# Two of the passes of a down-projection turned into seven-product block multiplication, in one weight stream with the up-projection

## The chip, the core and the metric

The kernel runs on one core of a Trainium2 chip. Its engines work at the same time, each through its own instructions in order: TensorE (PE in the rows) multiplies matrices, VectorE (DVE) and ScalarE (ACT) do elementwise work, GpSimd (POOL) does some elementwise work and issues some transfers, SyncE (SP) issues the other transfers. They wait for each other through semaphores. TensorE reads both operands from the on-chip buffer SBUF and adds its results up in PSUM, whose eight banks VectorE and ScalarE empty. The metric is the device time of one execution in microseconds (us); less is better.

## The reference, cut to what matters

One layer: a state-space group and a convolution group share an input and an output projection, and then a gated MLP with a short convolution follows. All in float32, 512 prompt tokens and 8 x 4 sample tokens, so 544 columns in all.

```python
D_MODEL = 2048
FFN_DIM = ((8 * D_MODEL // 3 + 127) // 128) * 128      # 5504 = 43 tiles of 128
def conv_ffn(h, buf0, w_up, conv_w, conv_b, w_down):
    u = h @ w_up
    u, buf = causal_dwconv(u, buf0, conv_w, conv_b)
    g, v = jnp.split(u, [FFN_DIM], axis=-1)
    return (jax.nn.silu(g) * v) @ w_down, buf
...
f, p_ffc = conv_ffn(rmsnorm(xp, norm_ffn_w[i]), p_ffc0, *ffn_w)
xp = xp + f
...
y_prompt = rmsnorm(xp, norm_final_w)
```

## The kernel before

Everything is held transposed: a tile is 128 features by 544 tokens, stored as two halves of 272 columns. Each float32 product is made from three matmuls. ScalarE rounds a weight block to a high part (`wh`, `sh`), VectorE or GpSimd subtracts to get the low part (`wl`, `sl`), and the input is split in the same way (`Ah`, `Al` and so on); then high x high, high x low and low x high are added up in PSUM. So one 128 x 128 weight tile against both halves of one input tile takes 6 matmuls of 272 columns.

The program is written out by hand in one order; nothing reorders it. It runs through: input projection, state-space and convolution groups, output projection (in `run_jobs`), then the up-projection, then the down-projection, then the final norm.

**Up-projection.** It has 43 groups; group g makes the gate tile and the value tile of feature block g together. The two weight rows (16 input tiles each) are seen as a 2 x 2 matrix of blocks of 8 tiles, the input as 2 x 2 blocks (8 tiles by 272 columns), and the product of the two is made with seven block products in place of eight (Strassen). I call one block product an *item*; its number in the stream is q, its number in its group m. The seven input combinations stand ready in `T_t` (`Ta`, `Th`, `Tl`). The weight combinations are made on the way: of five loads per group two come as a plain load on SP followed by an accumulating load on GpSimd's queue, which adds a second block to the first in SBUF (line 1207); two more sums are made by VectorE (`sum_a` line 1213, `sum_b` line 1217, tile `ws`). The loads sit in five buffers (`wr`). In item q the order is: ScalarE rounds the weights of item q + 2 (`prep_h`), VectorE empties the PSUM bank of item q - 1 (`evac`), a part of the convolution of the group before (`conv_task`), VectorE makes the low part of item q + 2 (`prep_l`), a sum or a load where one is due, and then the 24 matmuls of item q (lines 1250 to 1252). Three buffers for high and three for low parts (`whl`) hold items q, q + 1 and q + 2. Each group ends in a tile of the MLP's hidden layer, which goes to HBM (`ad`).

**Down-projection.** The pools of the up-projection are closed and others opened in their memory (`swap`). The 43 hidden tiles are taken in chunks of 14, 13, 12 and 4 (`CHUNKS`). For each of the first three, the tiles are loaded (`ar`) and split (`Ah`, `Al`, lines 1119 and 1120), and for each of the 16 output tiles the weights come in blocks of up to four tiles (`raw`, `wh`, `wl`, lines 117 and 118), run through `run_jobs` (matmuls on line 228, six for each weight tile), and the sum is added to the residual `xres` (line 1397). The last chunk of four goes through `last_half` with weights kept ready (`kh`, `kl`), one half of the columns after the other, so that the final norm of the first half can run beside the second.

Of the kernel before, what the change touches and what calls it, by code (L numbers as in the profile page):

```python
# [21 lines left out]
CHUNKS = [14, 13, 12, 4]  # L22
# [7 lines left out]
def hymba_step_kernel(ctx: ExitStack, tc: tile.TileContext, a: dict):  # L30
# [236 lines left out]
    with tc.manual_schedule():  # L267
# [833 lines left out]
        def ou_pre(i):  # L1101
            def f():
                if i == 0:
                    while not idle():
                        tick()
                    load_xr(0)
                if i + 1 < 16:
                    load_xr(i + 1)
                else:
                    delay(0, up_open)  # L1110
                    delay(0, lambda: (t_first(5), t_fourth(5)))
                    delay(1, lambda: (t_second(5), t_third(5)))
                    delay(1, lambda: (t_first(6), t_fourth(6)))
                    delay(2, lambda: (t_second(6), t_third(6)))
# [7 lines left out]
        def t_first(k):  # L1122
            t = slot("Ta", dt=F32R)
            split_into(t[:, 0, :], t[:, 1, :], xs[k][:, 0, :])
            T_t[0, k] = (t[:, 0, :], t[:, 1, :])

        def t_pair(k, src, ms):
            h, l = slot("Th", dt=F32R), slot("Tl", dt=F32R)
            split_into(h, l, src)
            for i, m in enumerate(ms):  # L1130
                T_t[m, k] = (h[:, i, :], l[:, i, :])

        tr = {}

        def t_second(k):
            p, q = xs[k], xs[k + 8]
            r = tr[k] = slot("tr")
            V.tensor_tensor(r[:, 1, :], p[:, 0, :], p[:, 1, :], ALU.subtract)
            V.scalar_tensor_tensor(r[:, 0, :], r[:, 1, :], -1.0, q[:, 1, :], ALU.mult, ALU.subtract)
            t_pair(k, r, (2, 3))  # L1140

        def t_third(k):
            p, q = xs[k], xs[k + 8]
            r, s = tr.pop(k), slot("tr")
            V.tensor_tensor(s[:, 0, :], q[:, 1, :], p[:, 1, :], ALU.subtract)
            V.scalar_tensor_tensor(s[:, 1, :], r[:, 0, :], -1.0, q[:, 0, :], ALU.mult, ALU.subtract)
            t_pair(k, s, (4, 6))

        def t_fourth(k):
            t_pair(k, xs[k + 8], (1, 5))  # L1150

        T_STEPS = [t_first, t_fourth, t_second, t_third]
        NPRE = 5

        def ou_evac(i):
            t = OT[i]

            def go(ps):
# [18 lines left out]
                if i % 2 and i // 2 < NPRE:  # L1177
                    steps += [lambda f=f: f(i // 2) for f in T_STEPS]
# [9 lines left out]

        KW = 8 * 128
        raw, wq, wr = {}, {}, None  # L1190

        def up_open():
            nonlocal wr
            wr = swap("wr", "side0", bufs=1, side="right")
            for j in (0, 1, 3, 2, 4):
                load_w(0, j)

        def load_w(g, j):
            if g >= HID:
                return  # L1200
            lo, hi = wup[g], wup[HID + g]
            src = (lo[:, 0:KW], hi[:, 0:KW], lo[:, 0:KW], lo[:, KW:2 * KW], hi[:, KW:2 * KW])[j]
            more = (None, hi[:, KW:2 * KW], hi[:, 0:KW], None, None)[j]
            t = wr.tile([128, KW], F32, tag="r", bufs=5, name=nm("wr"))
            Y.dma_start(out=t, in_=src)
            if more is not None:
                G.dma_start(out=t, in_=more, accum_op=ALU.add)  # L1207
            raw[g, j] = t

        def sum_a(g):  # L1210
            if g < HID:
                raw[g, 5] = wr.tile([128, KW], F32, tag="s", bufs=1, name=nm("ws"))
                V.tensor_tensor(raw[g, 5], raw[g, 1], raw[g, 0], ALU.add)
                load_w(g + 1, 0)

        def sum_b(g):
            V.tensor_tensor(raw[g, 5], raw[g, 5], raw[g, 3], ALU.add)
            load_w(g + 1, 3)

        def prep_h(q):  # L1220
            g, m = divmod(q, 7)
# [412 lines left out]
```

## Time and profile before

| what | value |
|---|---|
| time, median of 3 runs | 2891.84 us (2891.19 to 2894.03) |
| time of the profiled execution | 2892.68 us |
| span of the profiled execution, first to last instruction | 2890.9 us |
| TensorE busy | 2837.0 us, 98% of the span, 22502 matmuls |
| VectorE busy | 1933.7 us, 67% |
| ScalarE busy | 1170.8 us, 40% |
| GpSimd busy | 882.5 us, 31% |
| mean granted TensorE clock | 0.992 of full speed |

Matmuls are pipelined: a matmul's recorded 289 ns covers its way through the array, and the next one starts long before it ends. What a matmul costs is therefore read from the distance of starts, or from the number of matmuls in a stretch without idle time. The profiled execution took 0.84 us more than the median.

### The profile page before, as it was taken

The page shows a single profiled execution, that of the slowest core. Times are in us where ns is not written, and L with a number is a line of the kernel's source. Part 1 is how long each engine was busy: PE and PEld are TensorE (multiplying, and loading weights), DVE is VectorE, ACT ScalarE, POOL GpSimd, SP SyncE. Part 2 cuts the span into 40 slices and gives each one's busy share as a digit, 9 for nine tenths or more (in the row PEclk, how much of TensorE's full clock was granted, in tenths as well). Part 3 has the DMA queues.
Part 4 walks back from the last instruction along what each step waited for, and adds up shares of the span by engine and source line. Part 5 has one row for each costly group of instructions (what it writes and reads, how often), then busy time and mean ns, then how long its engine had stood idle before and what let it go on. Part 6 is the DMA issues. An engine that isn't in the chain of part 4 may idle for free. (4 is left out here: it accounts for less than half of the span.)

```text
span 2890.9 us, 55668 instructions
## 1 busy us (share of the span) xinstructions
PE 2837.0 (98%) x22502; PEld 2796.8 (97%) x22502; DVE 1933.7 (67%) x2912; ACT 1170.8 (40%) x1768; POOL 882.5 (31%) x896
## 2 busy tenths in 40 slices
PE   8999999999999999999999999999999989999997
PEld 7999998999999999999899999999999989999997
DVE  7576665777777778244598888888888863242335
ACT  4545444333333424233344444444444442232224
POOL 4466657667676655401100000000000000000003
PEclk9999999999999999999999999999999999999999
DMA  4243342433333343444476767777677764343521
GB/s 162 83 122 103 90 141 91 128 107 105 103 97 94 102 153 117 142 134 133 142 186 184 198 184 192 191 189 193 185 195 186 193 202 133 105 134 90 152 80 63
DMA packets 196674, 403.43 MB, mean 140 GB/s; under 512 B 38336, under 2 KB 47168, under 8 KB 196416
## 3 DMA queue, kind: packets, MB, share of 16 engines
q1 hardware_dynamic: 184032, 354.78, 40.0%
q0 software_dynamic: 12384, 45.09, 8.0%
q8 instruction: 176, 2.88, 0.4%
q14 instruction: 82, 0.67, 0.1%
HBM read 357.37 MB, written 42.41 MB: 138 GB/s over the span
## 5 line engine op out<-in xcount | busy, mean ns | idle before, releaser
L117 ACT CAST wh<-raw 128x512 fp32r<-128x512 f32 x592 | 355.6, 603 | 867.7 <-PE mm L228 743.7
L1250 PE MATMUL st<-Th,sh 128*128 128x272 f32 x2064 | 596.1, 289 | 1.5 <-ACT sh L1226 1.5
L1252 PE MATMUL st<-Th,sl 128*128 128x272 f32 x2064 | 595.8, 289 | 1.1 <-DVE sl L1235 1.1
L1251 PE MATMUL st<-Tl,sh 128*128 128x272 f32 x2064 | 595.7, 289 | 0.0
L118 POOL TENSOR_TENSOR wl<-raw,wh 128x512 fp32r<-128x512 f32 x336 | 449.9, 1341 | 422.8 <-ACT wh L117 362.6
L228 PE MATMUL mm<-xh,wh 128*128 128x272 f32 x2304 | 487.5, 293 | 7.5 <-ACT xh L312 7.5
L228 PE MATMUL mm<-xl,wh 128*128 128x272 f32 x2304 | 479.5, 289 | 4.5 <-DVE xl L314 4.5
L228 PE MATMUL mm<-xh,wl 128*128 128x272 f32 x2304 | 478.5, 289 | 0.0
L118 DVE TENSOR_TENSOR wl<-raw,wh 128x512 fp32r<-128x512 f32 (+2 forms) x256 | 180.4, 707 | 354.0 <-ACT wh L117 349.3
L1250 PEld LDWEIGHTS st<-Th,sh 128*128 128x128 f32 x2064 | 388.5, 188 | 1.7 <-ACT sh L1226 1.7
L1252 PEld LDWEIGHTS st<-Th,sl 128*128 128x128 f32 x2064 | 388.5, 188 | 1.5 <-DVE sl L1235 1.5
L1251 PEld LDWEIGHTS st<-Tl,sh 128*128 128x128 f32 x2064 | 388.5, 188 | 0.0
L228 PEld LDWEIGHTS mm<-xh,wh 128*128 128x128 f32 x2304 | 365.6, 189 | 20.5 <-issue 10.4
L228 PEld LDWEIGHTS mm<-xl,wh 128*128 128x128 f32 x2304 | 365.4, 188 | 6.0 <-DVE xl L314 6.0
L228 PEld LDWEIGHTS mm<-xh,wl 128*128 128x128 f32 x2304 | 365.4, 188 | 0.0
L1226 ACT CAST sh<-wr 128x1024 fp32r<-128x1024 f32 x215 | 225.4, 1049 | 272.6 <-PE st L1251 262.2
L1207 POOL DMA_DIRECT2D wr<-in_w_up x86 | 74.9, 871 | 828.9 <-DVE pu L1267 534.3
L937 DVE SCALAR_TENSOR_TENSOR ax<-w,cfw,ax 128x512 f32<-128x512 f32 x448 | 302.2, 747 | 5.8 <-ACT ax L913 5.8
L1235 DVE TENSOR_TENSOR sl<-wr,sh 128x1024 fp32r<-128x1024 f32 x215 | 262.5, 1221 | 40.4 <-ACT sh L1226 40.3
L228 PE MATMUL mm<-Ah,wh 128*128 128x272 f32 x1248 | 260.3, 290 | 7.5 <-ACT Ah L1119 7.5
L228 PE MATMUL mm<-Al,wh 128*128 128x272 f32 x1248 | 260.2, 290 | 0.0
L228 PE MATMUL mm<-Ah,wl 128*128 128x272 f32 x1248 | 260.1, 289 | 0.0
(299 smaller groups left out, 4965.8 us busy)
## 6 DMA issues: line engine op xcount, KB each, us to landing
wr<-in_w_up SPq DMA_DIRECT2D x215, 512.0 KB, 4.6
raw<-in_w_in SPq DMA_DIRECT2D x292, 256.0 KB, 3.2
wr<-in_w_up POOLq DMA_DIRECT2D x86, 512.0 KB, 9.2
raw<-in_w_down SPq DMA_DIRECT2D x144, 256.0 KB, 2.7
raw<-in_w_out SPq DMA_DIRECT2D x128, 256.0 KB, 2.9
ad<-ra SPq DMA_DIRECT2D x43, 272.0 KB, 6.9
ar<-ad SPq DMA_DIRECT2D x43, 272.0 KB, 4.1
h<-in_h SPq DMA_DIRECT2D x32, 256.0 KB, 3.5
```

The lines of the kernel that those rows point to most:

```text
L117: S.copy(h[:, :n], r[:, :n])
L118: (cur["wl"] or eng).tensor_tensor(l[:, :n], r[:, :n], h[:, :n].bitcast(F32), ALU.subtract)
L228: T.matmul(o, lhsT=w[:, c], rhs=x[:, hf, :], start=first, stop=last)
L937: V.scalar_tensor_tensor(p, w[:, i:i + 512], wt(i), p, ALU.mult, ALU.add)
L1207: G.dma_start(out=t, in_=more, accum_op=ALU.add)
L1226: S.copy(h, src)
L1235: V.tensor_tensor(l, src, h.bitcast(F32), ALU.subtract)
L1250: T.matmul(out, lhsT=h[:, c], rhs=xh_, start=k == 0, stop=False)
L1251: T.matmul(out, lhsT=h[:, c], rhs=xl_, start=False, stop=False)
L1252: T.matmul(out, lhsT=l[:, c], rhs=xh_, start=False, stop=k == 7)
```

## The change

The weights of the up- and the down-projection become one stream of items through the same buffers (`wr`, `whl`) and PSUM banks (`pst`); the pools are no longer swapped between them. A `Group` is seven items with five loads, as the up-projection had them; a `Plain` is one item of the ordinary kind: one output tile, K weight tiles, both halves, two PSUM banks. `DOWN = [(6, 6), (5, 6), (4, 0)]` replaces `CHUNKS`: a plain pass over 6 hidden tiles (16 items, one for each output tile), then a pass of eight groups over 12 hidden tiles (6 pairs; a group makes output tiles t and t + 8), a plain pass over 5, eight groups over the next 12, a plain pass over 4, and `last_half` over the last 4 as before. So 24 tiles go through block products and 15 through plain passes.

A group's products are added straight to the residual (`down_evac`, scratch tile `pd`). The seven input combinations of a pair of hidden tiles (`prep_pair`, formerly `t_first` to `t_fourth`) are made during the plain pass ahead (`pairs_prep`). Loads of hidden tiles, residual tiles and kept weights hang on item numbers (`at_item`). The program keeps a count of free load buffers (`free`), and each buffer that falls free takes the next load of the whole stream (`issue`). Of a group's five loads the order is now 0, 1, 3, 2, 4 throughout; before, load 2 went ahead of load 3 from the second group on.

```diff
-CHUNKS = [14, 13, 12, 4]
+DOWN = [(6, 6), (5, 6), (4, 0)]
...
+        class Group:
+            def __init__(self, lo, hi, K, T, evac):
+                n = K * 128
+                self.a = (lo[:, 0:n], lo[:, n:2 * n], hi[:, 0:n], hi[:, n:2 * n])
+                self.K, self.T, self.evac, self.q = K, T, evac, len(items)
+                items.extend((self, m) for m in range(7))
+                loads.extend((self, j) for j in (0, 1, 3, 2, 4))
+                sums[self.q - 1] = lambda: sum_a(self)
+                sums[self.q + 2] = lambda: sum_b(self)
+
+        class Plain:
+            def __init__(self, src, K, rhs, evac):
...
+        def issue(n=0):
+            free[0] += n
+            while free[0] and loads:
+                free[0] -= 1
+                o, j = loads.popleft()
+                src, more = o.a, None
+                if type(o) is Group:
+                    a11, a12, a21, a22 = o.a
+                    src, more = ((a11, None), (a21, a22), (a11, a21), (a12, None), (a22, None))[j]
+                t = wr.tile([128, KW], F32, tag="r", bufs=5, name=nm("wr"))[:, 0:o.K * 128]
+                Y.dma_start(out=t, in_=src)
+                if more is not None:
+                    G.dma_start(out=t, in_=more, accum_op=ALU.add)
+                raw[o, j] = t
...
-            if m in (3, 4, 6):
-                load_w(g + 1, {3: 1, 4: 2, 6: 4}[m])
+            if m in (None, 3, 4, 6):
+                issue(1)
...
+            outs = [pst.tile([128, 512], F32, tag="st", name=nm("st"))[:, 0:NH] for _ in range(2 if m is None else 1)]
+            bank[q] = outs
+            if m is None:
+                mms(outs, (0, 1), h, l, o.K, 0, o.K, o.rhs)
+                return
...
-        swap(None, "wr")
-        Cur.side = swap("side2", bufs=NSIDE, side="right")
-        Cur.wp = swap("wp2", "whl", bufs=1)
-        Cur.pmm = swap("pmm2", "pst", bufs=2, space=bass.MemoryType.PSUM)
...
+        def a_prep(ks, q):
+
+            for i, k in enumerate(ks):
+                at_item(q + i - 2, lambda k=k: a_load(k))
+                at_item(q + i, lambda k=k: a_split(k))
...
+        def plain_evac(t):
+            def f(m, *os):
+                for hf, o in enumerate(os):
+                    V.tensor_tensor(xres[t][:, hf, :], o, xres[t][:, hf, :], ALU.add)
+            return f
+
+        def down_evac(t):
...
+                elif m == 1:
+                    V.tensor_tensor(x[:, 0, :], o, x[:, 0, :], ALU.add)
+                    V.tensor_tensor(x[:, 0, :], x[:, 0, :], p[:, 0, :], ALU.add)
+                elif m == 2:
+                    V.tensor_tensor(p[:, 0, :], o, p[:, 0, :], ALU.add)
+                elif m == 3:
+                    V.tensor_tensor(p[:, 1, :], o, p[:, 0, :], ALU.add)
+                    V.tensor_tensor(x[:, 1, :], x[:, 1, :], p[:, 1, :], ALU.add)
+                elif m == 4:
+                    V.tensor_tensor(p, o.unsqueeze(1).to_broadcast([128, 2, NH]), p, ALU.add)
+                    V.tensor_tensor(y, y, p, ALU.subtract)
...
+        def down_group(k0, n, T):
+            for t in range(8):
+                w = [wdn[i, :, k0 * 128:(k0 + 2 * n) * 128] for i in (t, t + 8)]
+                Group(w[0], w[1], n, T, down_evac(t))
+
+        def pairs_prep(k0, n, T, q, step):
+
+            for i in range(n):
+                b = q + int(step * i)
+                for k in (k0 + i, k0 + n + i):
+                    at_item(b, lambda k=k: a_load(k))
+                st = prep_pair(T, i, lambda i=i: ar[k0 + i], lambda i=i: ar[k0 + n + i])
+                for f, d in zip(st, (2, 2, 3, 4)):
+                    at_item(b + d, f)
+                at_item(b + 4, lambda i=i: (ar.pop(k0 + i), ar.pop(k0 + n + i)))
...
+        for c, (n, pn) in enumerate(DOWN):
+            q = len(items)
+            a_prep(range(k0, k0 + n), q - n + 1)
+            down_plain(k0, n)
...
+            if pn:
+                pairs_prep(k0, pn, T_d[c], q, 11 / (pn - 1))
+                down_group(k0, pn, T_d[c])
+                k0 += 2 * pn
...
+        keep_prep(ktail, ntail, len(items) - 16)
```

Three places where the order of the instructions moves. The first is SP's queue, which issues the transfers, at the end of the up-projection. Names: `wr` and `raw` are weight buffers, `ar` a hidden tile read back from its HBM copy `ad`, `out_o_ffc` and `ad<-ra` are stores of the last groups. Before:

```order
L1205 DMA wr_27467<-in_w_up 128x1024
L179 DMA out_o_ffc<-w_27311 128x50
L179 DMA out_o_ffc<-w_27426 128x50
L179 DMA ad_221<-ra_27498 128x544
L179 DMA out_o_ffc<-w_27563 128x50
L101 DMA raw_27805<-in_w_down 128x512
L101 DMA raw_27811<-in_w_down 128x512
L101 DMA raw_27817<-in_w_down 128x512
L101 DMA raw_27823<-in_w_down 128x256
L101 DMA raw_27829<-in_w_down 128x512
L1377 DMA ar_27831<-ad_181 128x544
```

And in the changed kernel at the same place:

```order
L1224 DMA wr_27467<-in_w_up 128x1024
L179 DMA out_o_ffc<-w_27311 128x50
L1224 DMA wr_27535<-in_w_down 128x768
L1363 DMA ar_27572<-ad_181 128x544
L179 DMA out_o_ffc<-w_27426 128x50
L1363 DMA ar_27610<-ad_182 128x544
L1224 DMA wr_27614<-in_w_down 128x768
L1363 DMA ar_27650<-ad_183 128x544
L1224 DMA wr_27654<-in_w_down 128x768
L1224 DMA wr_27657<-in_w_down 128x768
L179 DMA ad_221<-ra_27498 128x544
```

The first weights of the down-projection and the first hidden tiles now stand among the stores of the last two up groups, and no longer behind all of them.

The second is VectorE in the down-projection where the input of the second block pass is prepared. Before, in the same stretch of the down-projection (the second chunk), low parts of weights and of the next hidden tiles alternate, with one addition to the residual for each output tile:

```order
L1397 TENSOR_TENSOR xres_28160<-mm_28162,xres_28160 128x544
L1120 TENSOR_TENSOR Al_28286<-ar_28226,Ah_28285 128x544
L118 TENSOR_TENSOR wl_28295<-raw_28264,wh_28294 128x256
L1120 TENSOR_TENSOR Al_28325<-ar_28258,Ah_28324 128x544
L118 TENSOR_TENSOR wl_28331<-raw_28292,wh_28330 128x512
```

In the changed kernel, two items of the plain pass over 5 tiles (`tr` holds differences of hidden tiles, `Ta`, `Th` and `Tl` the input of the block products):

```order
L1383 TENSOR_TENSOR xres_27967<-st_30471,xres_27967 128x272
L1383 TENSOR_TENSOR xres_27967<-st_30472,xres_27967 128x272
L1144 TENSOR_TENSOR tr_30507<-ar_30327,ar_30325 128x272
L1145 SCALAR_TENSOR_TENSOR tr_30507<-tr_30460,ar_30327 128x272
L1119 TENSOR_TENSOR Tl_30511<-tr_30507,Th_30510 128x544
L1119 TENSOR_TENSOR Ta_30514<-ar_30416,Ta_30514 128x272
L1119 TENSOR_TENSOR Tl_30518<-ar_30418,Th_30517 128x544
L1258 TENSOR_TENSOR sl_30525<-wr_30297,sh_30503 128x640
L1383 TENSOR_TENSOR xres_28034<-st_30529,xres_28034 128x272
L1383 TENSOR_TENSOR xres_28034<-st_30530,xres_28034 128x272
```

Five more instructions stand between one item's emptying of its two banks and the low part `sl` of the item after next.

The third is VectorE in a down-projection group. Before, every output tile of a chunk had this pattern:

```order
L1397 TENSOR_TENSOR xres_29247<-mm_31023,xres_29247 128x544
L118 TENSOR_TENSOR wl_31131<-raw_31114,wh_31130 128x128
L118 TENSOR_TENSOR wl_31161<-raw_31128,wh_31160 128x512
L118 TENSOR_TENSOR wl_31191<-raw_31158,wh_31190 128x512
L118 TENSOR_TENSOR wl_31221<-raw_31188,wh_31220 128x512
```

Now, from the fifth product of one group to the second of the next (line 1236 is `sum_a`):

```order
L1405 TENSOR_TENSOR pd_28824<-st_28913,pd_28824 128x544
L1406 TENSOR_TENSOR xres_28282<-xres_28282,pd_28824 128x544
L1258 TENSOR_TENSOR sl_28936<-wr_28757,sh_28932 128x768
L1408 TENSOR_TENSOR xres_27817<-st_28938,xres_27817 128x272
L1258 TENSOR_TENSOR sl_28960<-wr_28856,sh_28957 128x768
L1236 TENSOR_TENSOR ws_28962<-wr_28828,wr_28757 128x768
L1410 SCALAR_TENSOR_TENSOR xres_28282<-st_28966,xres_28282 128x272
L1258 TENSOR_TENSOR sl_28988<-ws_28962,sh_28985 128x768
L1258 TENSOR_TENSOR sl_29013<-wr_28828,sh_29009 128x768
```

`sum_a` reads `wr_28828`, the load with an accumulating part, and the low part of the same buffer, two instructions on, is what frees it for the next group's accumulating load.

## Rows read from the trace of the kernel before

**Rows 1.** The page, its head and part 1: span, busy us and share of each engine.

```profile
span 2890.9 us, 55668 instructions
...
PE 2837.0 (98%) x22502; PEld 2796.8 (97%) x22502; DVE 1933.7 (67%) x2912; ACT 1170.8 (40%) x1768; POOL 882.5 (31%) x896
```

**Rows 2.** The page, part 5: groups of matmuls; count, busy, mean ns, idle before.

```profile
L1250 PE MATMUL st<-Th,sh 128*128 128x272 f32 x2064 | 596.1, 289 | 1.5 <-ACT sh L1226 1.5
...
L228 PE MATMUL mm<-Ah,wh 128*128 128x272 f32 x1248 | 260.3, 290 | 7.5 <-ACT Ah L1119 7.5
```

**Rows 3.** Busy time in two stretches: up-projection, down-projection; instructions touched (x), clock, DMA share.

```profile
core 0: us, PE busy (x) PEld busy (x) DVE busy (x) ACT busy (x) POOL busy (x), PEclk, DMA share, GB/s
1800.00:2300.00 500.00, 500.00 (x3972) 500.00 (x3971) 435.06 (x639) 239.13 (x308) 41.14 (x48) 1.00 0.72 191
2400.00:2600.00 200.00, 200.00 (x1581) 200.00 (x1580) 69.50 (x114) 51.73 (x95) 0.00 (x0) 1.00 0.41 117
```

**Rows 4.** TensorE's waits from 2200 us to the end: in total, times, longest.

```profile
PE mm L228 <- ACT Ah L1119: 7.5, 1, 7.5
```

**Rows 5.** TensorE in order of time at the switch: start, length, count, idle before.

```profile
2339.48 0.29 PE L1252 MATMUL st<-Th,sl 128*128 128x272 f32 x1
2347.28 0.82 PE L228 MATMUL mm<-Ah,wh 128*128 128x272 f32 x2 [7.51 <-ACT Ah L1119]
...
2352.74 0.65 PE L228 MATMUL mm<-Ah,wl 128*128 128x272 f32 x2
...
2354.43 0.41 PE L228 MATMUL mm<-Al,wh 128*128 128x272 f32 x2
```

**Rows 6.** SP's queue and ScalarE at the switch, in order of time.

```profile
2339.68 2.24 SPq L101 DMA_DIRECT2D raw<-in_w_down  x5
...
2346.59 0.64 ACT L1119 CAST Ah<-ar 128x544 fp32r<-128x544 f32 x1 [0.71 <-DMA ar<-ad]
```

**Rows 7.** VectorE and ScalarE in one up group, in order of time.

```profile
2275.38 1.22 DVE L1213 TENSOR_TENSOR ws<-wr,wr 128x1024 f32<-128x1024 f32 x1
2276.52 0.43 DVE L1275 TENSOR_TENSOR c<-st,c 128x272 f32<-128x272 f32 x1
2276.88 0.69 DVE L1285 TENSOR_TENSOR w<-c,rr 128x512 f32<-128x512 f32 x1
...
2276.71 1.05 ACT L1226 CAST sh<-ws 128x1024 fp32r<-128x1024 f32 x1 [2.50 <-DVE ws L1213]
```

**Rows 8.** VectorE preparing a pair of input tiles ahead of the up-projection, in order of time.

```profile
1408.20 0.71 DVE L1120 TENSOR_TENSOR Tl<-xs,Th 128x544 fp32r<-128x544 f32 x1
1408.84 0.43 DVE L1138 TENSOR_TENSOR tr<-xs 128x272 f32<-128x272 f32 x1
...
1410.51 0.73 DVE L1120 TENSOR_TENSOR Tl<-tr,Th 128x544 fp32r<-128x544 f32 x1 [0.77 <-ACT Th L1119]
1411.15 0.43 DVE L1145 TENSOR_TENSOR tr<-xs,xs 128x272 f32<-128x272 f32 x1
```

**Rows 9.** Transfers of the up-projection: line 1205 on SP, line 1207 on GpSimd, issue to landing.

```profile
2260.57 4.30 SPq L1205 DMA_DIRECT2D wr<-in_w_up  x3
...
2264.96 0.86 POOL L1207 DMA_DIRECT2D wr<-in_w_up  x1 [16.65 <-DVE pu L1267]
...
L1207 POOL DMA_DIRECT2D wr<-in_w_up x48: 862/865/888, 1799.4 to 2289.5; - x48
...
DMA to landing us min/median/max: 7.9/9.2/10.7
...
L1205 SPq DMA_DIRECT2D wr<-in_w_up x117: 327/328/696, 1804.9 to 2297.8; - x117
...
DMA to landing us min/median/max: 3.5/4.6/8.9
```

**Rows 10.** The page, part 6: transfers by line, KB each, median us to landing.

```profile
raw<-in_w_down SPq DMA_DIRECT2D x144, 256.0 KB, 2.7
...
ar<-ad SPq DMA_DIRECT2D x43, 272.0 KB, 4.1
```

More of the change, by code (lines that the diff above doesn't have):

```diff
@@ L1194, in up_open, with sum_a, sum_b, prep_h @@
             wr = swap("wr", "side0", bufs=1, side="right")
[L1195 to L1199, printed above, removed]
[L1200 to L1225 removed]
+            issue()
+        def sum_a(o):
+            raw[o, 5] = wr.tile([128, KW], F32, tag="s", bufs=1, name=nm("ws"))[:, 0:o.K * 128]
+            V.tensor_tensor(raw[o, 5], raw[o, 1], raw[o, 0], ALU.add)
+            issue(1)
+        def sum_b(o):
+            V.tensor_tensor(raw[o, 5], raw[o, 5], raw[o, 3], ALU.add)
+            issue(1)
+        def prep_h(q):
+            if q >= len(items):
+                return
+            o, m = items[q]
+            src = raw[o, 0 if m is None else (0, 3, 5, 1, 2, 5, 4)[m]]
+            h = whl.tile([128, KW], F32R, tag="h", bufs=3, name=nm("sh"))[:, 0:o.K * 128]
             S.copy(h, src)
@@ L1240, in hymba_step_kernel @@
-        bank = {}
+            if m in (None, 3, 4, 6):
+                issue(1)
         def product(q):
-            g, m = divmod(q, 7)
+            o, m = items[q]
             h, l = wq.pop(q)
-            bank[q] = pst.tile([128, 512], F32, tag="st", name=nm("st"))
-            out = bank[q][:, 0:NH]
-            for k in range(8):
-                xh_, xl_ = T_t[m, k]
-                c = slice(k * 128, k * 128 + 128)
-                T.matmul(out, lhsT=h[:, c], rhs=xh_, start=k == 0, stop=False)
-                T.matmul(out, lhsT=h[:, c], rhs=xl_, start=False, stop=False)
-                T.matmul(out, lhsT=l[:, c], rhs=xh_, start=False, stop=k == 7)
@@ L1401, in hymba_step_kernel @@
+        a_prep(range(ktail, HID), len(items) - 16)
         fin = {}
@@ L1523, in hymba_step_kernel @@
-        run_jobs()
+        run_jobs()
+        whl = swap("whl", "wp", bufs=1)
+        pst = swap("pst", "pmm", bufs=4, space=bass.MemoryType.PSUM)
+        x7 = x_pair(7)
+        prep_h(0)
+        prep_l(0)
+        drain_later()
+        x7[0]()
+        prep_h(1)
+        fcw = cload("fcw", [128, 86, 4])
+        fstate = []
+        for i in range(3):
+            n = min(29, 86 - 29 * i)
+            fstate.append(slot("fs", [128, 29, 16]))
+            Y.dma_start(out=fstate[i][:, 0:n, :], in_=a["ffn_state"][:, 29 * i:29 * i + n, :])
@@ new lines, in hymba_step_kernel @@
+        for q in range(len(items)):
+            tick()
+            if q == 0:
+                x7[1]()
+                prep_l(1)
+                x7[2]()
+                sums[-1]()
+            prep_h(q + 2)
+            if q:
+                evac(q - 1)
+            for fn in tasks.pop(q, []):
+                fn()
+            prep_l(q + 2)
+            if q == 1:
+                x7[3]()
+                xs.clear()
+            if q in sums:
+                sums[q]()
+            product(q)
```

268 lines of the change are left out of this document (110 added, 158 removed).

## The prediction, made before the changed kernel was run

> **What bounds the kernel now.** I read the busy times first: TensorE is busy for 98% of the span, no other engine for more than 67% [rows 1]. A busy TensorE need not be at its best, so I counted matmuls in two stretches without idle time. In the up-projection 3972 are touched in 500 us; two of them lie across the edges, so one costs 500 / 3970 = 0.1259 us. In the down-projection it is 200 / 1579 = 0.1267 us. Both are at full clock [rows 3]. The waits say the same from the other side: in the last 690 us TensorE waits for an operand long enough to notice only once, 7.5 us for the first hidden tile of the down-projection [rows 2, 4]; the up-projection's largest group of matmuls shows 1.5 us of idle time over all its 2064 [rows 2]. So here time is the number of matmuls, plus that one place. A saved matmul is saved time as long as VectorE, ScalarE and the transfers keep two items ahead; that is what has to be checked.
>
> **Part 1, the matmuls.** 24 hidden tiles leave the plain form: 24 tiles x 6 matmuls x 16 output tiles = 2304, at 0.1267 us [rows 3] 291.9 us. They come back as 2 passes x 8 groups x 7 products x 6 tiles x 3 = 2016. These are the same lines and the same one-bank form as in the up-projection, so I take its 0.1259 us: 253.9 us. The difference is -38 us. At the plain rate the new ones cost 255.4 us, and the difference would be -36.5 us; these are the two ends. The other 1440 plain matmuls and the 384 of the last four tiles stay.
>
> **Part 2, the switch.** From the last up matmul at 2339.48 us to 2354.43 us there are 33 starts (one, then 16 rows of two), which at full rate take 33 x 0.126 = 4.2 us; they took 14.95 us [rows 5]. So the switch costs 10.8 us: 7.5 us of idle time, and the rest because the first matmuls after it start 5.46 / 24 = 0.23 us apart [rows 5], which is the 1.2 GHz level of the clock after an engine that stood still, against 0.126 us at 2.4 GHz. The cause is order: SP issues the first down weights at 2339.68 us, just after the last up matmul, the hidden tiles come behind them, and the first `Ah` is rounded at 2346.59 us [rows 6]. In the changed kernel nothing is swapped: the first weights stand among the stores of the last up groups, and the first six hidden tiles are loaded in items 294 to 299 and split two items later. Two up items are 2 x 24 x 0.126 = 6.0 us; such a load lands in 4.1 us [rows 10]. Splitting adds one 544-column instruction on VectorE per item, 0.64 us by the distance of starts [rows 8]. VectorE was busy 87% there [rows 3], 2.63 of 3.02 us, so it falls behind by 0.25 us in each of six items, 1.5 us in all, against a lead of one item and more. I take -10.8 us. If the cover fails, this term goes to nothing.
>
> **Part 3, VectorE in the plain passes.** An item of the 6-tile pass lasts 36 x 0.1267 = 4.56 us, of the 5-tile pass 3.80 us. By distances of starts a 272-column instruction takes 0.36 us and a 1024-column one 1.14 us [rows 7], a 544-column one 0.64 us [rows 8]; on the line between the last two, 640 columns take 0.74 and 768 take 0.87 us. Two steps of the preparation of a pair (`second`, `third`) are each two 272-column differences, a wait for ScalarE of 0.77 us and a 544-column subtraction; the trace has one of them, 2.31 us from 1408.84 to 1411.15 us [rows 8]. The other two steps are 0.36 + 0.64. A pair is 5.6 us, one comes every 2.2 items, and each item brings two evacuations (0.72 us) and a low part. First pass: 5.6 + 2.2 x 1.59 = 9.1 us in 10.0 us of matmuls; the last convolution takes some 4.6 us more in the first six items, once. It keeps up. Second pass: 5.6 + 2.2 x 1.46 = 8.8 us in 8.4 us: behind by 0.4 us a pair, some 2 us after five. What waits for it first are the PSUM banks: item q + 1 needs those of q - 1, so VectorE may be behind by 3.80 - 0.72 = 3.1 us. In items in which two steps meet it is about a microsecond further behind. So the stall is from nothing to 3.6 us: the upper end takes recorded lengths (0.44, 0.73, 0.84 us) with no overlap, which makes 9.7 us a pair, 5 x 1.3 - 3.1 after five. I take +1 us, as distances of starts are what this engine did when it was behind. It can't be a gain, since the matmuls are not fewer for it.
>
> **Part 4, the groups.** A group item is 18 matmuls, 2.27 us, a group 15.9 us. VectorE: seven low parts and two sums at 0.87, seven 272-column and two 544-column instructions, 7.8 + 2.5 + 1.3 = 11.6 us. ScalarE has seven roundings of about 0.8 us. Both fit, no cost.
>
> The narrow place is a loop through the accumulating load: the plain load lands, GpSimd adds the second block, `sum_a` uses the buffer, ScalarE rounds the sum, VectorE makes two low parts, and the second of these frees a buffer for the next group's accumulating load. In the up-projection the plain load was issued at 2260.57 us and the accumulation began at 2264.96 us, 4.4 us later; such a one takes 9.2 us (7.9 to 10.7) to land [rows 9], so at 2274.2 us; `sum_a` began at 2275.38 us [rows 7]. That is 1.2 us in hand, in a group of 21.2 us. The blocks are now 384 KB, not 512, but the group is 15.9 us, and a part of a transfer's time does not shrink. Bounds for the plain load are 2.7 us at 256 KB [rows 10] and 4.6 us at 512 KB [rows 9], I take 3.6. For the accumulation they are 9.2 us unscaled and 6.9 us scaled by size; I take 8.0. The rest is 0.87 + 0.8 + 2 x 0.87 and some 0.1 of hand-over, 3.5 us, with ScalarE's 1.05 us scaled [rows 7]. The loop is 15.1 us, between 13.1 and 17.3, against 15.9. So it costs nothing at the value that I take. Where it is longer, the excess comes seven times in each pass, less a stock of about 2.3 us (a low part is due 4.5 us after its item's turn begins and takes 2.2). At 17.3 us: 2 x (7 x 1.4 - 2.3) = 15 us.
>
> The Trainium skill has a rule for such a transfer ("DMA: Bandwidth & Descriptors", section "Anatomy of one DMA — SWDGE (gpsimd) path"): about 2.0 us fixed plus the bytes at 436 GB/s. By it the accumulation takes 2.9 us as an estimate from that page, the loop 10 us, and the time would be the same as my sum. This trace does not bear the rule out, with 7.9 us at the least for 512 KB [rows 9].
>
> Transfers are no bound: a group moves 7 x 0.393 MB in 15.9 us, 173 GB/s; the up-projection ran at 191 GB/s without a wait [rows 3]. The tail after the last matmul, the up-projection and all ahead of it keep their work. The swapped order of loads 2 and 3 comes after the load that the loop needs.
>
> **Sum.** 2892.68 - 37.9 - 10.8 + 1.0 = 2845.0 us for the profiled execution, which was 0.84 us over the median: 2844 us.
>
> **Rivals.** (a) The accumulating loads set the pace of the groups. For it: 1.2 us in hand before, and a period shorter by a quarter. Against it: smaller blocks and fewer other transfers. At a loop of 16.8 us it costs 2 x (7 x 0.9 - 2.3) = 8 us: 2852 us; at the end 2859 us. (b) VectorE comes late in the plain passes by the upper bound: 3.6 in place of 1.0, 2847 us. (c) The change doesn't do all that it says: the stream still stops at the switch, because `Ah` or the first weights come late behind the stores in SP's queue. Then the 10.8 us stay: 2855 us. (d) Slower than before: loads in the groups collide. At the longest landings of the trace, 8.9 and 10.7 us [rows 9], the loop is 23.1 us, the excess 7.2 us, and 2 x (50 - 2.3) = 96 us are added: 2940 us. It ends above the old time from an excess of 3.8 us, a loop of 19.7 us on average in place of 15.1. Such landings were the worst of 117 and of 48, not their mean.
>
> **How the numbers follow.** Forecast (2841 to 2848 us) 0.66, (b) 0.08, (a) 0.16, (c) 0.06, (d) 0.03, and 0.01 for none of these. The range 2841 to 2856 us takes in the forecast with both ends of part 1, all of (b), (c), and about half of (a), some 0.88; that is no more than the ends of the unknown costs need. A measurement of this kernel can tell about 0.2%, 6 us, from no change. All cases but (d) and the far end of what I can't name are faster by more: faster 0.96, within 0.2% 0.01, slower 0.03.
>
> **What would show it.** Part 1: 2016 matmuls on the group lines of the down-projection, 126 ns apart, and 288 matmuls fewer in all. Part 2: no wait for `Ah`, and no fall of the clock at the end of the up-projection. Part 3: short waits of TensorE late in the second plain pass, for VectorE. Rival (a): waits that grow through a block pass and end with it, VectorE idle ahead of `sum_a` until an accumulating load. Rival (c): one wait of several microseconds at the first plain item. I am wrong if TensorE's idle time in the down-projection adds up to more than some 10 us, or if matmuls in the groups are further apart than 0.127 us with no wait ahead of them.

## The result and the profile after

The changed kernel takes 2846.41 us (median of 4 runs, 2844.91 to 2849.48), the kernel before 2891.73 us beside it: a ratio of 0.9843 with a 95% interval of 0.9826 to 0.9860, so 45.3 us less. The forecast was 2844 us with a range of 2841 to 2856 us.

The page of the changed kernel, head and part 1, answers to [rows 1]. TensorE has 288 matmuls fewer, and VectorE 164 us more work:

```profile
span 2847.7 us, 55491 instructions
...
PE 2798.8 (98%) x22214; PEld 2758.7 (97%) x22214; DVE 2097.4 (74%) x3192; ACT 1214.4 (43%) x1792; POOL 910.8 (32%) x928
```

TensorE's waits from 2200 us to the end (total, times, longest) answer to [rows 4]. The one wait of 7.5 us is gone, and four kinds of short waits stand in its place:

```profile
PE st L1276 <- DVE sl L1258: 0.8, 2, 0.4
PE ax L1487 <- POOL sq L1520: 0.4, 1, 0.4
PE st L228 <- ACT Ah L1118: 0.4, 1, 0.4
PE st L228 <- DVE Al L1119: 0.2, 1, 0.2
```

Busy time in the first block pass and in the second plain pass answers to [rows 3]: TensorE is busy throughout, VectorE in 78% and 79% of it, at full clock.

```profile
core 0: us, PE busy (x) PEld busy (x) DVE busy (x) ACT busy (x) POOL busy (x), PEclk, DMA share, GB/s
2417.00:2544.00 127.00, 127.00 (x1009) 127.00 (x1009) 99.16 (x147) 51.11 (x68) 12.21 (x14) 1.00 0.71 176
2544.20:2605.00 60.80, 60.80 (x482) 60.80 (x482) 47.98 (x98) 24.88 (x41) 1.74 (x2) 1.00 0.56 161
```

The page's part 6 (KB each, median us from issue to landing) has the new accumulating loads, which stand on GpSimd's queue: 5.7 us at 384 KB. No such size was in the trace of before.

```profile
wr<-in_w_up POOLq DMA_DIRECT2D x86, 512.0 KB, 8.2
wr<-in_w_down SPq DMA_DIRECT2D x96, 384.0 KB, 3.4
...
wr<-in_w_down POOLq DMA_DIRECT2D x32, 384.0 KB, 5.7
```

Where the time went is easiest to see by stage. The table is worked out from starts of matmuls in the profiled executions: the first of the up-projection, its last, the first on a hidden tile (`Ah`), the first of the last four tiles, and the end of the span. Ahead of the up-projection nothing was changed, yet the profiled executions of this study reach it between 1417.67 and 1421.29 us, the changed kernel last; the comparison therefore starts there. A second profiled execution of the changed kernel (e8, below) takes 1426.58 us from there on.

| us | before | after | e1 (stream only) | e2 (late tiles) | e5a (order) |
|---|---|---|---|---|---|
| up-projection | 920.23 | 921.55 | 922.08 | 920.00 | 920.23 |
| switch, to the first `Ah` | 7.80 | 0.13 | 0.13 | 5.45 | 0.13 |
| first 39 hidden tiles | 477.33 | 437.67 | 474.40 | 438.99 | 436.53 |
| last 4 tiles and end | 66.31 | 67.08 | 66.75 | 67.46 | 67.08 |
| together | 1471.67 | 1426.43 | 1463.36 | 1431.90 | 1423.97 |

Before to after it is -45.2 us: 7.7 at the switch, 39.7 in the 39 tiles, and two losses, 1.3 in the up-projection and 0.8 at the end.

### The profile page after: what moved, and what is told of

Same layout as the page of the kernel before. It is cut to its first block, busy times and chain, and to the rows that moved or that the text cites. A ratio compares the mean times of both kernels' runs of the same rounds, so it can differ in the third digit from the quotient of the medians.

```text
span 2847.7 us, 55491 instructions
## 1 busy us (share of the span) xinstructions
PE 2798.8 (98%) x22214; PEld 2758.7 (97%) x22214; DVE 2097.4 (74%) x3192; ACT 1214.4 (43%) x1792; POOL 910.8 (32%) x928
## 5 line engine op out<-in xcount | busy, mean ns | idle before, releaser
L1276 PE MATMUL st<-Th,sl 128*128 128x272 f32 x2640 | 762.4, 289 | 1.5 <-DVE sl L1258 1.5
L1274 PE MATMUL st<-Th,sh 128*128 128x272 f32 x2640 | 762.5, 289 | 1.5 <-ACT sh L1249 1.5
L1275 PE MATMUL st<-Tl,sh 128*128 128x272 f32 x2640 | 762.0, 289 | 0.0
L1249 ACT CAST sh<-wr 128x1024 fp32r<-128x1024 f32 (+3 forms) x343 | 327.1, 954 | 415.9 <-PE st L1275 338.9
L1276 PEld LDWEIGHTS st<-Th,sl 128*128 128x128 f32 x2640 | 496.9, 188 | 2.4 <-DVE sl L1258 2.4
L1274 PEld LDWEIGHTS st<-Th,sh 128*128 128x128 f32 x2640 | 496.9, 188 | 1.7 <-ACT sh L1249 1.7
L1275 PEld LDWEIGHTS st<-Tl,sh 128*128 128x128 f32 x2640 | 497.0, 188 | 0.0
L1258 DVE TENSOR_TENSOR sl<-wr,sh 128x1024 fp32r<-128x1024 f32 (+3 forms) x343 | 378.0, 1102 | 55.1 <-ACT sh L1249 55.0
L228 PEld LDWEIGHTS mm<-xh,wh 128*128 128x128 f32 x2304 | 366.0, 189 | 20.4 <-issue 10.6
L1249 ACT CAST sh<-ws 128x1024 fp32r<-128x1024 f32 (+1 forms) x118 | 117.1, 992 | 259.3 <-DVE ws L1236 144.7
L1258 DVE TENSOR_TENSOR sl<-ws,sh 128x1024 fp32r<-128x1024 f32 (+1 forms) x118 | 136.0, 1153 | 31.3 <-ACT sh L1249 22.0
```

The lines of the kernel that those rows point to most:

```text
L228: T.matmul(o, lhsT=w[:, c], rhs=x[:, hf, :], start=first, stop=last)
L1249: S.copy(h, src)
L1258: V.tensor_tensor(l, src, h.bitcast(F32), ALU.subtract)
L1274: T.matmul(outs[0], lhsT=h[:, c], rhs=xh_, start=k == 0, stop=False)
L1275: T.matmul(outs[0], lhsT=h[:, c], rhs=xl_, start=False, stop=False)
L1276: T.matmul(outs[0], lhsT=l[:, c], rhs=xh_, start=False, stop=k == o.K - 1)
```

## Experiments on the two gains

**e1, the shared stream without block products.**

```diff
-DOWN = [(6, 6), (5, 6), (4, 0)]
+DOWN = [(8, 0), (8, 0), (8, 0), (8, 0), (7, 0)]
...
-        T_d = [{}, {}]
+        T_d = [{} for _ in DOWN]
```

> The shared stream alone: all 39 hidden tiles ahead of the last four go in plain passes (8, 8, 8, 8, 7 tiles), no block products. The theory says that the change is two gains that add: 288 matmuls fewer in the groups (38 us, of which none is given back) and a switch without its stop (8.3 of 10.8 us in the profile of the changed kernel). So this kernel keeps only the second: 2891.7 - 8.3 = 2883 us (2880 to 2887, as 80 items in five passes have other evacuations than three passes), with the same 22502 matmuls as before. Rival 1, the stream is worth nothing by itself, or costs what it saves: 2892. Rival 2, the switch is worth more than the gap that is seen in it, and the block products less: 2870 or below.

Measured: 2885.40 us (9 runs, 2882.57 to 2888.91), ratio 0.9976 (0.9966 to 0.9986), 7.4 us under before beside it. By stage it is 8.3 us under before. The 22502 matmuls are all there:

```profile
PE 2834.6 (98%) x22502; PEld 2795.7 (97%) x22502; DVE 1952.3 (68%) x2928; ACT 1151.7 (40%) x1672; POOL 883.4 (31%) x896
```

So the two gains add, as the theory had it. The same 39 tiles take 474.40 us here and 437.67 us in the changed kernel: the block products are worth 36.7 us, and 37.9 us against e5a, which has the block products without the small waits at the switch. 477.33 - 474.40 = 2.9 us is what the low clock behind the stop cost before (granted clock 0.50 from 2347.3 to 2352.7 us).

**e2, the first hidden tiles late.** The first six are loaded and split in the item that uses them.

```diff
-            a_prep(range(k0, k0 + n), q - n + 1)
+            if c == 0:
+                for k in range(n):
+                    at_item(q, lambda k=k: a_load(k))
+                for k in range(n):
+                    at_item(q, lambda k=k: a_split(k))
+            else:
+                a_prep(range(k0, k0 + n), q - n + 1)
```

> The changed kernel, but the first six hidden tiles are loaded and split in the item of their first use, instead of six items ahead. The theory says that the stop at the switch came from this order alone and not from the pools that were swapped: it returns with a wait of 6 to 8 us for the first hidden tile and a stretch at the lower clock behind it, 8 to 10 us in all, less the 2.5 us of small waits that the early splits cost: 2846.4 + 6 to 8 = 2853 to 2855 us. Rival, the swap of pools (or the first weights behind the stores) was the cause: no change, 2846 us.

Measured: 2853.73 us (4 runs, 2853.26 to 2854.14), ratio 0.9863 (0.9847 to 0.9880). TensorE and ScalarE of this kernel at the switch, in order of time (start, length, instruction, count, idle before):

```profile
2340.05 0.29 PE L1276 MATMUL st<-Th,sl 128*128 128x272 f32 x1
2345.50 0.82 PE L228 MATMUL st<-Ah,sh 128*128 128x272 f32 x2 [5.16 <-ACT Ah L1118]
...
2347.34 0.65 PE L228 MATMUL st<-Ah,sh 128*128 128x272 f32 x2
2347.79 0.66 PE L228 MATMUL st<-Al,sh 128*128 128x272 f32 x2
...
2344.81 4.18 ACT L1118 CAST Ah<-ar 128x544 fp32r<-128x544 f32 x6 [2.33 <-DMA ar<-ad]
```

The stop is back, with the pools not swapped: ScalarE waits for the hidden tile's transfer, TensorE for ScalarE. Behind it two matmuls take 0.45 us, 0.23 us each, the same low level of the clock as in [rows 5]; the granted clock from 2345.5 to 2350 us is 0.50. The up-projection in front of it takes 920.00 us, so without early splits its small waits are gone too. The late hidden tiles alone are enough for a stop of 5.2 us. The old one was 7.5 us, with five weight loads (2.24 us of SP's queue, [rows 6]) ahead of the first hidden tile; no run separates these 2.3 us. By stage e2 lies 5.5 us over the changed kernel, less than the 7.3 us of the medians; some of the rest lies ahead of the up-projection, where the two kernels are the same.

**e5a and e5, what stayed at the switch.** First the changed kernel in item 297, VectorE and ScalarE, and then TensorE behind them:

```profile
2332.68 0.19 DVE L1317 TENSOR_TENSOR w<-c,nr 128x32 f32<-128x32 f32 x1
2334.50 0.72 DVE L1119 TENSOR_TENSOR Al<-ar,Ah 128x544 fp32r<-128x544 f32 x1 [1.63 <-ACT Ah L1118]
2335.15 1.22 DVE L1258 TENSOR_TENSOR sl<-ws,sh 128x1024 fp32r<-128x1024 f32 x1
...
2333.08 0.85 ACT L1319 ACTIVATE o<-w,fcw 128x560 f32<-128x560 f32 x1
2333.84 0.63 ACT L1118 CAST Ah<-ar 128x544 fp32r<-128x544 f32 x1
...
2335.71 0.29 PE L1275 MATMUL st<-Tl,sh 128*128 128x272 f32 x1
2336.42 0.39 PE L1276 MATMUL st<-Th,sl 128*128 128x272 f32 x1 [0.42 <-DVE sl L1258]
2336.64 0.29 PE L1274 MATMUL st<-Th,sh 128*128 128x272 f32 x1
```

VectorE makes the convolution's input until 2332.87 us. ScalarE works on it (L1319) and only then rounds the hidden tile. VectorE, whose next instruction is that tile's low part, stands still for 1.63 us. Behind it in VectorE's queue is the low part of the up weights, which TensorE needs. The edit changes the order alone: ScalarE rounds the hidden tile ahead of the convolution, and VectorE makes its low part behind that of the weights.

```diff
+        post = {}
+        def a_early(ks, q):
+            for i, k in enumerate(ks):
+                at_item(q + i - 2, lambda k=k: a_load(k))
+                def hi(k=k):
+                    Ah[k], Al[k] = slot("Ah", dt=F32R), slot("Al", dt=F32R)
+                    S.copy(Ah[k], ar[k])
+                def lo(k=k):
+                    V.tensor_tensor(Al[k], ar.pop(k), Ah[k].bitcast(F32), ALU.subtract)
+                tasks.setdefault(q + i, []).insert(0, hi)
+                post.setdefault(q + i, []).append(lo)
...
-            a_prep(range(k0, k0 + n), q - n + 1)
+            (a_prep if c else a_early)(range(k0, k0 + n), q - n + 1)
...
+            for fn in post.pop(q, []):
+                fn()
             product(q)
```

e5 has `q - n + bool(c)` in place of `q - n + 1`: the first pass one item earlier. e8 is the changed kernel again, on the same chip.

> The changed kernel unaltered, as the measure for the two kernels on the switch that run on the same chip. Both theories expect 2846 us (2844 to 2849), with two waits for low parts of up weights at the end of the up-projection, one for the sixth first-pass tile's Ah and one for its Al.

> The changed kernel with another order within the six items that split the first hidden tiles: ScalarE rounds the hidden tile ahead of the convolution's work, and VectorE makes its low part behind that of the up weights. The theory on the 2.5 us that stayed at the switch: VectorE stands still 1.5 us in each of these items for ScalarE's rounding, which stands behind a convolution instruction that in its turn waits for VectorE, and so the low part of the up weights comes late. Then the two waits for that low part go (about 1.3 us with what follows them) and the one for Ah; the one for Al of the sixth tile stays or grows, as it is made last in the item of its use. 1 to 2 us less than the changed kernel on the same chip: 2844 to 2845 us. Rival, VectorE has simply more work there than time (0.25 us an item, as in the prediction): the waits stay or only change their place, 2846 us.

> The same order, and the six hidden tiles one item earlier, so that the sixth is split in the item ahead of its use. The theory expects all four waits gone: 2.5 us less than the changed kernel on the same chip, 2843 to 2844 us, and the whole switch worth the 10.8 us of the prediction. Rival (too much work for VectorE): at least the waits for the up weights' low part stay, 2845 to 2846 us.

Measured: e8 2847.11 us (2846.25 to 2848.72), e5a 2844.61 us (2844.36 to 2844.86), e5 2845.79 us (2845.43 to 2846.03); to before 0.9842 (0.9828 to 0.9855), 0.9833 (0.9819 to 0.9846) and 0.9837 (0.9823 to 0.9850). These intervals overlap, since the runs of before spread more than the difference; the single runs of e8, e5a and e5 do not overlap. TensorE's waits in e5a from 2200 us to the end, and then VectorE's in e5a from 2320 to 2350 us:

```profile
PE ax L1502 <- POOL sq L1535: 0.4, 1, 0.4
```

```profile
DVE xres L1398 <- PE st L228: 3.1, 2, 1.8
DVE sl L1258 <- ACT sh L1249: 0.9, 2, 0.4
DVE c L1292 <- PE st L1276: 0.4, 1, 0.4
```

All waits at the switch are gone, the one for `Al` too, which I had expected to stay. VectorE has the same work as before the edit, and now waits for TensorE there: it is ahead. So it was not too much work, it was the order; which of the two moves did it, ScalarE's or VectorE's, was not run apart. e5a is the fastest kernel of this study, 2.5 us under e8 and 47.4 us under before. e5 misses its expectation by 1.8 us. Its matmuls run like those of e5a to the last one on a hidden tile; its last 18.9 us, from there on, are 1.0 us longer than in e5a. Why is open; nothing was edited there.

## Experiments on VectorE and on the accumulating loads

**e6, pairs prepared closer together.**

```diff
-                pairs_prep(k0, pn, T_d[c], q, 11 / (pn - 1))
+                pairs_prep(k0, pn, T_d[c], q, 7 / (pn - 1))
```

> The changed kernel, but the six pairs of hidden tiles are prepared 1.4 items apart instead of 2.2. The theory is the working of part 3: 5.6 us of VectorE for a pair and 1.46 to 1.59 us for an item, so 7.6 us in 5.3 us of matmuls in the second plain pass, behind by 2.3 us a pair, 11.5 us after five pairs, less the 3.1 us that VectorE may be late: 8 us; in the first pass 7.8 in 6.4 us, 7 us after five and some 4.6 us of convolution, less 3.8: 3 to 8 us. Together 2846.4 + 11 to 16 = 2857 to 2862 us, all of it as waits for VectorE in the two plain passes. Rival, those numbers are too large because ScalarE's and VectorE's work overlap more than I counted (no wait was seen in the changed kernel): under 2849 us.

Measured: 2860.99 us (4 runs, 2858.99 to 2863.05), ratio 0.9889 (0.9874 to 0.9903). The first plain pass grew from 74.10 to 79.39 us, the second from 60.79 to 68.99 us: 5.3 and 8.2 us, where 3 to 8 and 8 were expected. TensorE's waits there, first row:

```profile
PE st L228 <- DVE xres L1383: 8.4, 8, 1.7
```

TensorE waits for a bank until VectorE has emptied it, as part 3 said. Its times fit: VectorE's work and its allowed lateness of 3.1 us give what the second pass lost. Not all of that loss is waiting, since the granted clock of that pass is 0.98. The spacing that the change chose has a margin of less than 0.8 items.

**e7, the accumulating load twice.**

```diff
                     G.dma_start(out=t, in_=more, accum_op=ALU.add)
+                    if o.K < 8 and j == 1:
+                        G.dma_start(out=t, in_=more, accum_op=ALU.add)
```

> The changed kernel, but in the down groups the accumulating load that the first sum needs is issued twice, the second after the first has landed; so the second block counts twice in that sum (what is computed there is changed). This lengthens the loop through the accumulating load by one landing. The theory is the loop of part 4 with the durations of the changed kernel: 3.4 + 5.7 + 3.5 = 12.6 us, with the second landing 18.3 us, against a group of 15.9 us: 2.4 us for each of seven groups, less a stock of 2.3 us, twice: 29 us, so 2875 us (2865 to 2890), with waits of TensorE that return in each group. Rival 1, the loads run far enough ahead that no loop exists: 2846 us. Rival 2, the loop was already close to the period, as the prediction took it (15.1 us): 4.9 us for each group, 2 x (34 - 2.3) = 64 us, 2910 us.

Measured: 2882.85 us (4 runs, 2876.59 to 2884.32), ratio 0.9960 (0.9945 to 0.9975). The block passes grew from 127.08 to 144.70 and 147.03 us, 37.6 us together. In this kernel `sum_a` is line 1238, and the second load line 1228. First TensorE's waits, then `sum_a` in the first block pass (2410 to 2565 us), then GpSimd's queue:

```profile
PE st L1276 <- ACT sh L1251: 15.6, 10, 3.5
PE st L1278 <- DVE sl L1260: 6.4, 15, 0.8
```

```profile
L1238 DVE TENSOR_TENSOR ws<-wr,wr x8: 952/958/959, 2413.3 to 2543.5; 128x768 f32<-128x768 f32 x8
its engine sat idle before it (us, times) until:
  DMA wr<-in_w_down: 26.9, 7
```

```profile
2476.34 0.87 POOL L1226 DMA_DIRECT2D wr<-in_w_down  x1 [10.74 <-DVE pd L1402]
2482.73 0.86 POOL L1228 DMA_DIRECT2D wr<-in_w_down  x1 [5.53 <-DMA wr<-in_w_down]
```

Here the loop of part 4 is seen at work: VectorE stands still ahead of each of seven sums until the load has landed. The period is (2543.5 - 2413.3) / 7 = 18.6 us. The added load starts 2482.73 - 2476.34 = 6.4 us after the first, so the loop without it is 12.2 us, against 15.9 us for a group: some 3.7 us in hand. This is an estimate from a run in which the load is late. In the changed kernel the same chain is stretched, because ScalarE's roundings on the way wait for buffers that TensorE still reads (0.95 us at 2482.98 us), and the load lands only a little ahead of its sum, after 5.8 us at 2494.7 us:

```profile
2488.86 0.86 POOL L1226 DMA_DIRECT2D wr<-in_w_down  x1 [11.64 <-DVE pd L1400]
2496.02 0.95 DVE L1236 TENSOR_TENSOR ws<-wr,wr 128x768 f32<-128x768 f32 x1
```

That is 1.4 us, as before the change (1.2 us in part 4), with no wait in front of the sum. Rival 1 (no loop) and rival 2 (nearly at the period) both fall. The cost was 36.4 us rather than 29, since the loop is 0.3 us longer than taken and the stock ahead of it nearer to 0 than to 2.3 us: 2.7 x 7 = 18.9 us a pass, and 17.6 and 19.9 us were measured.

**e3, short groups.** With products of 3 tiles a group lasts 63 x 0.126 = 7.94 us, so the loop should come close.

```diff
-DOWN = [(6, 6), (5, 6), (4, 0)]
+DOWN = [(6, 3), (5, 3), (5, 3), (5, 0)]
...
-        T_d = [{}, {}]
+        T_d = [{} for _ in DOWN]
```

> The changed kernel with three passes of block products over 6 tiles each (18 in place of 24), each product 3 tiles long instead of 6, and four plain passes (6, 5, 5, 5 tiles) between. By the matmul term alone 1728 x 0.1267 - 1512 x 0.1259 = 28.6 us are saved instead of 37.9: 2846.4 + 9.3 = 2856 us. The theory of the loop adds to that: a group lasts 63 x 0.126 = 7.94 us, and the loop is estimated from rows of the changed kernel and of before (plain load 3.4 at 384 KB and 2.7 at 256 KB, accumulation 5.7 at 384 KB) as 2.2 + 2.9 to 4.5 + 1.9 = 7.0 to 8.6 us; VectorE has by its starts 7.8 us of work in a group. So nothing to 10 us of waits in the three passes: 2856 to 2866 us, from the point where a group is shorter than the loop. Rival, a transfer has a larger fixed part than that (accumulation near 5.5 us at any size): loop 9.6 us, 1.7 us a group, 3 x (7 x 1.7 - 1.1) = 32 us, 2888 us.

Measured: 2903.54 us (5 runs, 2899.34 to 2909.07), ratio 1.0036 (1.0024 to 1.0049): slower than before, and outside both expectations. The three block passes take 77.31, 76.06 and 76.95 us in place of 63.5 each, and the three plain passes of five tiles 65.28, 61.70 and 63.41 us in place of 60.8: 40 and 8 us more. TensorE waits for low parts, not for rounded sums:

```profile
PE st L1276 <- DVE sl L1258: 17.2, 28, 1.9
PE st L228 <- DVE sl L1258: 3.5, 3, 1.7
PE st L1274 <- ACT sh L1249: 2.5, 4, 0.9
```

The 8 us of the plain passes are not waits alone. Behind the waits of the block passes the clock fell: in the second plain pass (2492 to 2557 us, columns as above) the granted clock is 0.95, and TensorE stands still for only 1.7 of the 4.5 us lost:

```profile
2492.00:2557.00 65.00, 63.30 (x480) 63.08 (x479) 39.90 (x79) 20.06 (x32) 1.73 (x2) 0.95 0.40 113
```

Three more kernels start from this one: e3b has three of VectorE's sums fewer in a group, e3c is without the accumulating load that `sum_a` needs, and e3d has both edits.

```diff
# e3b and e3d
-                    V.tensor_tensor(x[:, 0, :], x[:, 0, :], p[:, 0, :], ALU.add)
...
-                    V.tensor_tensor(x[:, 1, :], x[:, 1, :], p[:, 1, :], ALU.add)
...
-                    V.tensor_tensor(y, y, p, ALU.subtract)
# e3c and e3d
-                if more is not None:
+                if more is not None and (o.K == 8 or j != 1):
```

> The short groups again, without three of VectorE's instructions in each group: the two 272-column and the one 544-column sum that add a product's share to the running output a second time (that part of the result is left out). The groups of that kernel lasted 9.2 to 9.7 us instead of 7.94. First theory: VectorE is the bound there; its 23 instructions take 8.1 us by their starts, and it stands still about 1 us in each group, for ScalarE's rounding of the sums and once or twice for the load. Without 1.36 us of work a group comes to 7.9 to 8.3 us: 24 x 1.36 = 32 us less, 2871 us (2866 to 2877). Rival, the loop through the accumulating load (3.9 us at 192 KB in that run): the period stays, 2900 to 2904 us.

> The short groups again, without the accumulating load that the first sum needs; the plain load of that buffer stays (so the second block is left out of that sum). This shortens the loop through the load by its landing, 3.9 us. First theory, VectorE is the bound: only the 3 to 4 us go that it was seen to wait for this load, 2899 to 2904 us. Rival, the loop was the bound: it is now 5 to 6 us, far under a group, and the 40 us of waits in the block passes go, 2860 to 2870 us.

> The short groups without both: the three sums in each group and the accumulating load for the first sum (so both parts of the computation are left out). Each alone left a group at 9.2 to 9.7 us instead of 7.94. Theory: two limits lie side by side in these groups, VectorE's queue with its waits for ScalarE (9.2 us, seen without the accumulating load) and the loop through that load (9.7 us, seen with fewer sums, where VectorE waits 2 us a group for it); taking away one leaves the other. With both away VectorE's queue comes to 9.2 - 1.4 = 7.8 us and no loop is near: the 40 us of the block passes and part of the 8 us of the plain passes go, 2856 to 2866 us. Rival, a third limit holds the groups (the lead of two short items between ScalarE, VectorE and TensorE, or the other accumulating load): 2880 us or more.

Measured: e3b 2906.12 us (ratio 1.0042, 1.0028 to 1.0056), e3c 2898.13 us (1.0020, 1.0011 to 1.0029), e3d 2882.76 us (0.9971, 0.9959 to 0.9982). e3b lies 2 us over the range of its rival, e3c 1 us under that of its first theory; e3d is where its rival put it. The starts of `sum_a` (line 1236) in the first block pass give the period of a group, for e3, e3b, e3c and e3d in this order; the row under that of e3b is what VectorE waited for ahead of it:

```profile
L1236 DVE TENSOR_TENSOR ws<-wr,wr x7: 548/551/560, 2424.2 to 2482.0; 128x384 f32<-128x384 f32 x7
```

```profile
L1236 DVE TENSOR_TENSOR ws<-wr,wr x7: 557/558/559, 2423.3 to 2481.3; 128x384 f32<-128x384 f32 x7
its engine sat idle before it (us, times) until:
  DMA wr<-in_w_down: 14.6, 7
```

```profile
L1236 DVE TENSOR_TENSOR ws<-wr,wr x7: 548/551/553, 2424.7 to 2479.8; 128x384 f32<-128x384 f32 x7
```

```profile
L1236 DVE TENSOR_TENSOR ws<-wr,wr x7: 548/549/552, 2422.3 to 2473.8; 128x384 f32<-128x384 f32 x7
```

Six distances each: 9.63, 9.67, 9.18 and 8.58 us. With fewer sums the period stays and VectorE waits 2.1 us a group for the load: the loop is 9.7 us. Without the load the period is 9.2 us, and VectorE waits for no load any more: its own queue, with its waits for ScalarE, is about as long. So two limits lie side by side, and each edit alone only uncovers the other; both together save 20.8 us of some 48 us. That is less than I expected of e3d; its rival, a third limit at 2880 us or more, holds. Its waits from 2415 to 2480 us:

```profile
DVE sl L1258 <- ACT sh L1249: 12.1, 22, 1.3
ACT sh L1249 <- PE st L1275: 11.7, 13, 1.2
```

VectorE waits for ScalarE's rounding and ScalarE for TensorE to give back a buffer, which would fit a lead of two items that is too short at 1.13 us an item. No kernel was run that tells it apart from the other accumulating load, so the last 20 us of the block passes of e3d stay open.

## Why the prediction was right, step by step

**Part 1, -37.9 us: right.** 474.40 us of e1 less 436.53 us of e5a is 37.9 us. The group matmuls stand 127.08 / 1008 = 0.1261 us apart in both block passes, and the plain ones of e1 474.40 / 3744 = 0.1267 us.

**Part 2, -10.8 us: the stop was sized right, its cover was not.** The stop cost 7.7 us of standing still and 2.9 us of low clock, 10.6 us in all, and e5a gets all of it back. The changed kernel gave back 2.5 us of it: 1.32 us with the waits for low parts in the last up items and 1.14 us with those for `Ah` and `Al` of the sixth tile. The four listed waits make 1.4 us of the 2.5 us. The rest is 0.26 us at each: a listed wait starts at the recorded end of the matmul before (0.29 us, where the next start would come after 0.13 us), and the first distance behind each stop is 0.23 us. The step that failed is that VectorE "falls behind by 0.25 us in each of six items, 1.5 us in all, against a lead of one item and more". It added up VectorE's instructions and left out a wait. The low part of a hidden tile also waits for ScalarE, and in three of the items this held VectorE's whole queue, 4.7 us together:

```profile
DVE Al L1119 <- ACT Ah L1118: 4.7, 3, 1.6
```

(VectorE's waits in the changed kernel, 2322 to 2352 us.) I had counted such a wait, 0.77 us, in the preparation of a pair, and left it out here, where the convolution's instruction ahead of `Ah` made it twice as long. The working has one slip that the 10.8 us do not rest on: up to 2352.74 us [rows 5] lie 22 distances and not 24, so the mean is 0.25 us; the first three are 0.37 to 0.39 us, those behind them 0.227 us.

**Part 3, +1.0 us: measured 0.** No wait stands in the second plain pass. The working itself gave "behind by 0.4 us a pair, some 2 us after five", against 3.1 us that VectorE may be late; so it gave 0, and the 1 us was a hedge towards the upper end. e6 shows that the working's numbers hold well where they are asked for 8.2 us. Rival (b), with recorded lengths and no overlap, falls.

**Part 4, 0 us: right, with a size that was off.** The accumulating load at 384 KB lands in 5.7 us, where I took 8.0 (bounds 6.9 and 9.2): below my lower bound, which scaled the median of [rows 9] by size; even the shortest landing there, 7.9 us, gives 5.9 us. Why it is shorter, no run shows. The loop is 12.2 us by e7 rather than 15.1. So rival (a) had some 3.7 us of room against it and not 0.8. That the loop is there, e7 shows. By the fit that the Trainium skill gives ("DMA: Bandwidth & Descriptors", section "Anatomy of one DMA — SWDGE (gpsimd) path") this load takes 2.9 us, as an estimate; the trace has 5.7 us, twice that.

**The rest.** Rival (c) is out, since e5a gets the whole stop back and the changed kernel most of it. Rival (d) was named for collisions, and its price was put at a loop of 19.7 us. What brings this design over the old time is another thing, a group that is shorter than its loop and VectorE's queue: e3. Against the sum, parts 2 and 3 were off by +2.7 and -1.0 us, and the end of the program was 0.8 us longer than before, which no step had; together +2.5 us on 2844 us, where 2846.4 us were measured. That errors of both signs met is luck, and so is an agreement to 0.1 us between runs that spread over 4.6 us.

## What to carry to other kernels

An engine's load in a stretch is not the sum of its instructions: where its next instruction waits for a partner engine, everything behind it in its queue waits too, so look for what the partner does first. Put work that nobody needs yet behind the work that somebody waits for, and round ahead of the long instruction, not behind it. Shorter blocks save fewer operations per load and shrink the period, while the chain of load, accumulation, sum and rounding keeps most of its length; work out that chain for the smallest block before choosing it.

## What was not expected of the hardware

The landing of an accumulating load does not go in proportion to its size: in the median 8.2 us at 512 KB, 5.7 us at 384 KB, and 3.9 us (e3) or 4.2 us (e3b, first block pass) at 192 KB, with other traffic beside each. Those of the up-projection took 8.2 us in the median where they took 9.2 us before, though their size and number are the same; the order of two loads in a group changed, but no run tells whether that is the cause.

A stop of 5.2 us in e2 was followed by matmuls at the lower of the two clock levels (granted clock 0.50), 0.23 us apart. A stop of 0.4 us in the changed kernel (at 2336.42 us) was followed by a single distance of 0.23 us and then by 0.126 us again, with a granted clock of 1.00 throughout: one long distance behind a stop is no sign of a lower clock.
